# Replicating rows over partitions in a hybrid encoder layer: the DMA or GpSimd

## The chip, the cores and the metric

The kernel runs on one core of one Trainium2 chip. The metric is the device time of one execution in microseconds (us); lower is better.

## What is computed

One post-norm layer on 1024 tokens of 1024 features: an input norm, a mixer (forgetting attention beside a gated linear recurrence), a gated feed-forward, a gated per-layer embedding, with a norm behind each. The change touches the input norm and one term of the attention; the reference for these two, cut:

```python
def layer_norm(x, g, b):
    mu = mean(x, -1); var = mean((x - mu)**2, -1)
    return (x - mu) * rsqrt(var + 1e-5) * g + b

h = layer_norm(x, ln_in_g, ln_in_b)                # (1024 tokens, 1024)
q, k, v, f, ... = split(h @ w_in)
logf = log_sigmoid(f + b_forget)                   # (tokens, 8 heads)
c = cumsum(logf, axis=tokens)
logit[t, s] = q_t . k_s / sqrt(128) + c[t] - c[s]  # s <= t, per head
out = softmax(logit) @ v
```

Everything is float32. Products are taken as three products of rounded halves (a high and a low part of each operand).

## The kernel before

Tokens or features lie on the 128 partitions, in tiles of 128 by up to 1024. Three rows must be the same on every partition: the gain `g` and the bias `b` of the input norm (feature vectors, used with tokens on the partitions) and, for each of the 8 heads, `c[s]` along the keys (`CB[h]`, 1024 numbers). All three are made in the same way before the change: a DMA brings one row of 4 KB into partition 0, and GpSimd's `partition_broadcast` copies it to all 128.

The program runs in stages, in this order:

- **Input norm and v** (0 to about 170 us). `norm(i)` (L571) normalizes token tile i: VectorE takes the statistics (L425, L401), GpSimd the root (L403, L405, L412), VectorE applies mean, gain and bias to the first 512 features (L418, L419), ScalarE (L414) and GpSimd (L415, L416) to the others; TensorE then transposes the tile (`to_fm`, L432). While the first tiles come in, `ple` (L519) multiplies the per-layer embedding (lines 317 to 320, evicted by ScalarE at L526), 16 units over 8 PSUM banks.
- **Recurrence, merge gates, q and k** (to about 650 us): `winograd` (L340), block products in `product` (L331). `Weights` splits raw weights ahead: GpSimd forms sums of two blocks (`prep`, L108), ScalarE and VectorE round them into halves (L126, L127). `QueryKey.query` (L809) and `MergeGates` (L792) evict banks on VectorE.
- **Attention** (about 650 to 900 us), 8 heads in 4 steps of 256 queries, 32 steps in all (L1006). In a step, `probs_t` (L962) transposes the probabilities (L972, TensorE), `scores` (L927) computes the products of the step after the next one (L939 to L943), `pv` (L977) multiplies with v (L280 to L282), and `br_unit` (L989, products at L291 to L294) runs a product of the recurrent branch in between. In `scores`, VectorE subtracts `CB[h]` and takes the maximum (L944), ScalarE takes the exponential and its sum (L955), VectorE the reciprocal (L957), and GpSimd scales each row (L959), which the transposes wait for. `load_c(h + 1)` (L922) is called in the first step of head h.
- **Branch products, mixer out, feed-forward, embedding gate, norms** (about 900 us to the end). Later norms get their rows by a replicating DMA that GpSimd issues (lines 1107, 1258 and 1325).

The order on each engine is set by the tile framework, which simulates the program while it builds it and lets instructions pass each other where their dependences allow it. Each engine then runs its own list in order, and a waiting instruction holds all that stands behind it. SP issues nearly all loads and most stores, ScalarE the stores of a few results. Two things around the change matter: `rows` (L475) are two places in `f_mem`, of which the first, at 0 KB, is also the first place of the ring of raw v weights (`v_raw`, L487); and the tiles of `CB` (L861) take turns at 20 and 24 KB of `f_mem`, where the recurrence has held its `ur` and `sq` tiles before (L674, L675).

Of the kernel before, what the change touches and what calls it, by code (L numbers as in the profile page):

```python
# [15 lines left out]
P = 128  # L16
# [16 lines left out]
def pair_ops(pairs, ahead):  # L33
    """The operands of products of 2x2 blocks in Winograd's form of Strassen's algorithm, in the order of use."""
    ops = []
    for a, _ in pairs[:ahead]:
        ops += [(0, a), (1, a)]
    for n, (a, b) in enumerate(pairs):
        nxt = pairs[n + ahead][0] if n + ahead < len(pairs) else None
        ops += [("S1", a, b), ("S2", a, b), ("S4", a, b)]  # L40
        ops += [(0, nxt)] if nxt is not None else []
        ops.append(("S3", a, b))
        ops += [(1, nxt)] if nxt is not None else []
        ops.append(("n", b))
    return ops


class Weights:
    """Splits a sequence of stationary operands into rounded halves ahead of their use.

    An op is (kind, raw, raw). Kinds 0 and 1 are the contraction halves of a block, "n" is the negated second
    half, "S1" to "S4" are the sums of the halves of two blocks that Winograd's form needs.
    """
# [95 lines left out]
    def give(self, n):  # L149
        """Gives n places of raw weights away as they get free, in given."""  # L150
        self.wanted = n
# [6 lines left out]
class Feed:  # L158
    """Loads run ahead of their use by the ring of raw tiles; items: (source, what to do with the tile)."""
# [21 lines left out]
class Ring:  # L181
    """Tiles by turns; those of first come before them once."""
# [12 lines left out]
def trunk(ctx, tc, A, out):  # L195
# [29 lines left out]
    # On-chip memory, offsets in KB. Slots of 16 KB: 0 to 6 hold rounded halves, 7, 8 and the two parts of 9 are  # L225
    # typed by phase; f_mem is float32.
# [22 lines left out]
    def sv(s, off, *shape):  # L249
        """A view at off in slot s."""  # L250
        if s == 9:
            return view(flex["9a" if off < 8 else "9b"], off % 8, shape)
        return view(flex[s], off, shape) if s in flex else view(r_mem, 16 * s + off, shape)

    def blk(s):
        """The halves of a [512, 512] block in slot s."""
        return sv(s, 0, 4, 512), sv(s, 8, 4, 512)
# [8 lines left out]
    def xs_of(slots):  # L266
        """Operand (k, token chunk) of a [1024, 1024] activation whose blocks lie in slots[2 * chunk + k // 4]."""
        def x(k, t):
            hi, lo = blk(slots[2 * t + k // 4])
            return hi[:, k % 4, :], lo[:, k % 4, :]  # L270
        return x

    def toks_of(slots, i):
        """The operands over k for token tile i."""
        x, o = xs_of(slots), i % 4 * P
        return [tuple(a[:, o:o + P] for a in x(k, i // 4)) for k in range(KC)]

    def mm3(bank, w, x, first, last):
        """bank += w.T @ x for pairs of halves."""
        nc.tensor.matmul(bank, lhsT=w[0], rhs=x[0], start=first, stop=False)  # L280
        nc.tensor.matmul(bank, lhsT=w[0], rhs=x[1], start=False, stop=False)
        nc.tensor.matmul(bank, lhsT=w[1], rhs=x[0], start=False, stop=last)  # L282

    def gemm_fm(w, x, kc, tcs=(0, 1)):
        """[128 features, 512 tokens] per token chunk, with the weights stationary; w(k): halves."""
        out = [psum() for _ in tcs]
        for k in range(kc):
            wh, wl = w(k)
            for b, t in zip(out, tcs):
                xh, xl = x(k, t)  # L290
                nc.tensor.matmul(b, lhsT=wh, rhs=xh, start=(k == 0), stop=False)  # L291
                nc.tensor.matmul(b, lhsT=wh, rhs=xl, start=False, stop=False)  # L292
            for b, t in zip(out, tcs):
                nc.tensor.matmul(b, lhsT=wl, rhs=x(k, t)[0], start=False, stop=(k == kc - 1))  # L294
        return out
# [8 lines left out]
    def w_gemm(x):  # L304
        """The next block of the weights times x."""
        b = gemm_fm(ent(W.take(2)), x, KC)
        W.free(2)
        return b

    def gemm_tm(xs, ws, widths):  # L310
        """[128 tokens, width] per width, with the activations stationary; xs, ws: lists over k."""
        out = [psum() for _ in widths]
        n = len(xs)
        for k in range(n):
            (xh, xl), w = xs[k], ws[k]
            for b, (wh, wl), n_ in zip(out, w, widths):
                nc.tensor.matmul(b[:, :n_], lhsT=xh, rhs=wh, start=(k == 0), stop=False)  # L317
                nc.tensor.matmul(b[:, :n_], lhsT=xh, rhs=wl, start=False, stop=False)  # L318
            for b, (wh, wl), n_ in zip(out, w, widths):
                nc.tensor.matmul(b[:, :n_], lhsT=xl, rhs=wh, start=False, stop=(k == n - 1))  # L320
        return out

    def product(bank, s, first, nk=4):
        """bank += the next operand of the weights times the block of slot s."""
        (e,) = W.take(1)
        hi, lo = blk(s)
        for k in range(nk):
            w = e[:, k * P:(k + 1) * P], e[:, 512 + k * P:512 + (k + 1) * P]
            for j, (a, x) in enumerate(((w[0], hi), (w[0], lo), (w[1], hi))):
                start, stop = first and k == 0 and j == 0, k == nk - 1 and j == 2  # L330
                nc.tensor.matmul(bank, lhsT=a, rhs=x[:, k, :], start=start, stop=stop, skip_group_check=not first)  # L331
        W.free(1)
# [7 lines left out]
    def winograd(pairs, blocks, ahead, prologue, new_tile):  # L340
        """Products of 2x2 blocks with seven block products each; pairs: what to do with the sums.

        The banks are read as sums of products grow in them: c11 = x + y, c12 = x + z, c22 = x + the p5 of z, c21 = x.
        The last pair has the last two products in banks of their own, and their sums in a tile.
        """
# [52 lines left out]
    def norm_stats(st):  # L398
        """1/sqrt(var + eps) and the mean of the collected halves."""
# [8 lines left out]
    def normalize(y, rs, mu, g, b, cut):  # L408
        """y = (y - mu) * rs * g + b, VectorE up to cut, ScalarE and GpSimd from there."""
# [11 lines left out]
    def layer_norm(y, g, b, cut=512):  # L421
        """y = LN(y) * g + b over the free axis."""
# [5 lines left out]
    def to_fm(src, s, o):  # L428
        """Transposes src [128 tokens, 512] into the block of slot s, at token o."""
# [10 lines left out]
    def late_sums(y, j):  # L440
        """In place: B22 - B12 for y[j + 4]'s first half, B22 - B12 + B11 and that - B21 for y[j]'s halves."""
# [13 lines left out]
    def log_sigmoid(t, x, res):  # L455
        """res = min(x, 0) - log1p(exp(-|x|)), by the series of artanh; t: scratch."""
# [14 lines left out]
    # ---- input norm; v and the forget gates, token-major; the per-layer embedding's product while they come in  # L471
# [3 lines left out]
    rows = [fv(0, D), fv(18.75, D)]  # L475
    g, b = fv(10.75, D), fv(14.75, D)
    for row, nm in zip(rows, ("ln_in_g", "ln_in_b")):
        nc.scalar.dma_start(row[0:1], A[nm])
# [55 lines left out]
    load_x(0)  # L534
    p_raws += [load_ple(1, 1), load_ple(0, 1)]
# [4 lines left out]
    for row, t in zip(rows, (g, b)):  # L540
        nc.gpsimd.partition_broadcast(t, row[0:1])
# [18 lines left out]
    # the first recurrence waits for the memory that h leaves, the last is over before attention begins  # L560
# [88 lines left out]
    # sums of the blocks of h  # L649
# [19 lines left out]
    # ---- recurrence, merge gates, q and k  # L669
# [7 lines left out]
    class Recurrence:  # L677
# [63 lines left out]
        def decay(self):  # L741
            # log_a = ns4 * (1 + ta); 1 - a^2 = tanh(-log_a) * (1 + a^2); a in xc from here on
# [112 lines left out]
    # ---- attention; the recurrent branch out runs between its steps  # L855
# [11 lines left out]
    def attention_memory():  # L867
# [7 lines left out]
        load_c(0, fv(12, S)[0:1])  # L875
# [46 lines left out]
    def load_c(h, row):  # L922
        nc.sync.dma_start(row, c_dram[h, :])
        CB[h] = cb_tile()
        nc.gpsimd.partition_broadcast(CB[h], row)

    def scores(h, c):  # L927
        mx = sm.tile([P, 2], F32, tag="mx", name="mx")
        scs = []
        for r in range(2):  # L930
# [4 lines left out]
            for s0, w in ((0, L),) if L <= 512 else ((0, 512), (512, L - 512)):  # L935
                # products of fewer than 256 columns would not be faster
# [11 lines left out]
        # the row's maximum, then what the exponent adds to q.k - c_s: c_t - max  # L948
# [57 lines left out]
    for s, (h, c) in enumerate(steps):  # L1006
# [8 lines left out]
        if c == 0 and h + 1 < H:  # L1015
            load_c(h + 1, sv(9, 8, S)[0:1])

    # ---- attention branch out and merge
# [62 lines left out]
    # ---- mixer out, norm  # L1081
# [37 lines left out]
    # the weights of the first half are in the way of the later blocks  # L1119
# [11 lines left out]
    # ---- feed-forward, in  # L1131
# [50 lines left out]
    def fill_block(g, m, js=None):  # L1182
        """Block m of group g: B11, B21, B12 - B11, B22 - B12 + B11, B22, B22 - B12, B22 - B12 + B11 - B21."""
# [37 lines left out]
    # ---- feed-forward, out  # L1221
# [6 lines left out]
    def quads(gi, j):  # L1228
        """Accumulators of token tiles j and j + 4, per half of the features."""
# [6 lines left out]
    # the gate's weights, split by halves of the features: some take what the last group leaves of the blocks' slots,  # L1236
    # the rest comes in as its blocks are done with
# [83 lines left out]
    # ---- gated per-layer embedding, norm  # L1321
# [101 lines left out]
```

## Time and profile before

| what | value |
| --- | --- |
| time, median of 3 runs | 1920.08 us (1917.54 to 1923.84) |
| span of the profiled execution | 1915.1 us |
| TensorE busy | 1800.3 us, 94% |
| VectorE, ScalarE, GpSimd busy | 1211.2, 814.4, 716.0 us |
| mean granted clock of TensorE | 0.973 of full speed |
| HBM traffic | 121 GB/s over the span |

The span runs from the first to the last instruction of one execution; the page gives no time of that execution beside it. The three times lie 2.4 to 8.7 us above the span, and the median 5.0 us. TensorE is the engine that is busy nearly all the time, so what matters is where it is idle, for whom it waits there, and where its clock is not at full speed.

### The profile page before, as it was taken

The page shows a single profiled execution, that of the slowest core. Times are in us where ns is not written, and L with a number is a line of the kernel's source. Part 1 is how long each engine was busy: PE and PEld are TensorE (multiplying, and loading weights), DVE is VectorE, ACT ScalarE, POOL GpSimd, SP SyncE. Part 2 cuts the span into 40 slices and gives each one's busy share as a digit, 9 for nine tenths or more (in the row PEclk, how much of TensorE's full clock was granted, in tenths as well). Part 3 has the DMA queues.
Part 4 walks back from the last instruction along what each step waited for, and adds up shares of the span by engine and source line. Part 5 has one row for each costly group of instructions (what it writes and reads, how often), then busy time and mean ns, then how long its engine had stood idle before and what let it go on. Part 6 is the DMA issues. An engine that isn't in the chain of part 4 may idle for free. (4 is left out here: it accounts for less than half of the span.)

```text
span 1915.1 us, 23685 instructions
## 1 busy us (share of the span) xinstructions
PE 1800.3 (94%) x8556; PEld 1506.5 (79%) x8556; DVE 1211.2 (63%) x1800; ACT 814.4 (43%) x1420; POOL 716.0 (37%) x635
## 2 busy tenths in 40 slices
PE   6999999999999689889999999999999989898897
PEld 4998878888888477778888878888888768686686
DVE  5644767666666565556545585454545687979887
ACT  4424556555566454445422144333433343333322
POOL 3622222223222232232000463343433573646665
PEclk8999999999999889989999999999999999899998
DMA  6632232222323533323734124222222256464322
GB/s 232 259 114 74 80 119 92 98 91 97 118 89 121 176 102 112 107 91 123 253 133 176 45 92 139 87 81 87 81 85 88 66 179 206 158 202 160 118 77 77
DMA packets 119497, 233.96 MB, mean 122 GB/s; under 512 B 10946, under 2 KB 49986, under 8 KB 119380
## 3 DMA queue, kind: packets, MB, share of 16 engines
q1 hardware_dynamic: 102240, 205.70, 32.4%
q10 hardware_dynamic: 16132, 23.08, 3.3%
q0 software_dynamic: 1008, 3.67, 0.5%
q8 instruction: 67, 1.10, 0.2%
q14 instruction: 50, 0.41, 0.1%
HBM read 162.12 MB, written 70.29 MB: 121 GB/s over the span
## 5 line engine op out<-in xcount | busy, mean ns | idle before, releaser
L331 PE MATMUL bank<-r_mem,s 128*128 128x512 f32 x3261 | 773.6, 393 | 27.6 <-DVE f_mem L1271 9.9
L331 PEld LDWEIGHTS bank<-r_mem,s 128*128 128x128 f32 x3261 | 614.6, 189 | 160.6 <-issue 8.1
L108 POOL TENSOR_TENSOR f_mem<-f_mem 128x512 f32<-128x512 f32 (+1 forms) x232 | 333.6, 1449 | 645.5 <-DVE s L127 219.1
L127 DVE TENSOR_TENSOR s<-f_mem,s 128x512 fp32r<-128x512 f32 (+1 forms) x280 | 235.8, 854 | 143.7 <-ACT s L126 125.0
L126 ACT CAST s<-f_mem 128x512 fp32r<-128x512 f32 (+1 forms) x280 | 169.5, 618 | 338.2 <-PE bank L331 198.6
L331 PE MATMUL bank<-r_mem 128*128 128x512 f32 x1131 | 277.6, 394 | 14.2 <-DVE f_mem L1167 6.6
L331 PEld LDWEIGHTS bank<-r_mem 128*128 128x128 f32 x1131 | 214.4, 190 | 62.8 <-DVE f_mem L1167 7.0
L317 PE MATMUL bank<-r_mem 128*128 128x344 f32 (+2 forms) x389 | 138.7, 357 | 0.5 <-ACT f_mem L526 0.4
L318 PE MATMUL bank<-r_mem 128*128 128x344 f32 (+2 forms) x389 | 136.8, 352 | 0.0
L320 PE MATMUL bank<-r_mem 128*128 128x344 f32 (+2 forms) x389 | 133.5, 352 | 0.6 <-DVE r_mem L264 0.6
L126 ACT CAST r_mem<-f_mem 128x512 fp32r<-128x512 f32 (+1 forms) x100 | 60.0, 607 | 143.5 <-PE bank L331 87.0
L127 DVE TENSOR_TENSOR r_mem<-f_mem,r_mem 128x512 fp32r<-128x512 f32 (+1 forms) x100 | 92.0, 926 | 30.8 <-ACT r_mem L126 30.3
L291 PE MATMUL bank<-r_mem,s 128*128 128x512 f32 x224 | 87.8, 392 | 0.0
L292 PE MATMUL bank<-r_mem,s 128*128 128x512 f32 x224 | 87.3, 390 | 0.0
L1167 DVE TENSOR_TENSOR f_mem<-f_mem,bank 128x512 f32<-128x512 f32 x21 | 14.4, 687 | 113.4 <-PE bank L331 113.4
L959 POOL TENSOR_SCALAR f_mem<-f_mem,rinv 128x128 f32<-128x128 f32 (+3 forms) x64 | 49.3, 782 | 95.2 <-DVE rinv L957 50.8
L264 DVE TENSOR_TENSOR r_mem<-bank,r_mem 128x512 fp32r<-128x512 f32 (+2 forms) x120 | 67.5, 593 | 26.2 <-ACT r_mem L263 26.1
L263 ACT CAST r_mem<-bank 128x512 fp32r<-128x512 f32 (+2 forms) x120 | 57.4, 518 | 61.0 <-PE bank L972 31.5
L294 PE MATMUL bank<-r_mem,s 128*128 128x512 f32 x224 | 82.2, 390 | 0.0
L317 PEld LDWEIGHTS bank<-r_mem 128*128 128x128 f32 x389 | 73.1, 188 | 8.3 <-ACT f_mem L526 0.8
L320 PEld LDWEIGHTS bank<-r_mem 128*128 128x128 f32 x389 | 73.1, 188 | 8.2 <-DVE r_mem L264 0.9
L318 PEld LDWEIGHTS bank<-r_mem 128*128 128x128 f32 x389 | 73.1, 188 | 7.0
(280 smaller groups left out, 3037.2 us busy)
## 6 DMA issues: line engine op xcount, KB each, us to landing
f_mem<-in_w_fg SPq DMA_DIRECT2D x22, 512.0 KB, 3.9
f_mem<-in_w_fu SPq DMA_DIRECT2D x22, 512.0 KB, 3.1
act_dram<-f_mem SPq DMA_DIRECT2D x43, 256.0 KB, 2.3
f_mem<-act_dram SPq DMA_DIRECT2D x16, 512.0 KB, 4.4
y_dram<-f_mem SPq DMA_DIRECT2D x32, 256.0 KB, 4.4
f_mem<-y_dram SPq DMA_DIRECT2D x26, 256.0 KB, 2.5
s<-in_w_ffn_out SPq DMA_DIRECT2D x12, 512.0 KB
f_mem<-in_w_ffn_out SPq DMA_DIRECT2D x10, 512.0 KB, 5.6
```

The lines of the kernel that those rows point to most:

```text
L108: self.nc.gpsimd.tensor_tensor(out, x, y, op=op)
L126: nc.scalar.copy(hi, src)
L127: nc.vector.tensor_tensor(lo, src, hi.bitcast(F32), op=ALU.subtract)
L263: nc.scalar.copy(hi, src)
L264: (eng or nc.vector).tensor_tensor(lo, src, hi.bitcast(F32), op=ALU.subtract)
L291: nc.tensor.matmul(b, lhsT=wh, rhs=xh, start=(k == 0), stop=False)
L292: nc.tensor.matmul(b, lhsT=wh, rhs=xl, start=False, stop=False)
L294: nc.tensor.matmul(b, lhsT=wl, rhs=x(k, t)[0], start=False, stop=(k == kc - 1))
L317: nc.tensor.matmul(b[:, :n_], lhsT=xh, rhs=wh, start=(k == 0), stop=False)
L318: nc.tensor.matmul(b[:, :n_], lhsT=xh, rhs=wl, start=False, stop=False)
L320: nc.tensor.matmul(b[:, :n_], lhsT=xl, rhs=wh, start=False, stop=(k == n - 1))
L331: nc.tensor.matmul(bank, lhsT=a, rhs=x[:, k, :], start=start, stop=stop, skip_group_check=not first)
```

## The change

The row of partition 0 and the copy by GpSimd go. One DMA for each row, with a source that repeats the row 128 times, writes all partitions: 512 KB into SBUF in place of 4 KB. For `g` and `b` ScalarE issues it, now behind `load_x(0)`; for `CB[h]` SP does. The rest of the diff takes out comments, and line numbers shift by up to 4.

```diff
     hs = (0, 1, 2, 3)
-    rows = [fv(0, D), fv(18.75, D)]
     g, b = fv(10.75, D), fv(14.75, D)
-    for row, nm in zip(rows, ("ln_in_g", "ln_in_b")):
-        nc.scalar.dma_start(row[0:1], A[nm])
...
     load_x(0)
+    for t, nm in ((g, "ln_in_g"), (b, "ln_in_b")):
+        nc.scalar.dma_start(t, A[nm].partition_broadcast(P))
...
-    for row, t in zip(rows, (g, b)):
-        nc.gpsimd.partition_broadcast(t, row[0:1])
...
-        load_c(0, fv(12, S)[0:1])
+        load_c(0)
...
-    def load_c(h, row):
-        nc.sync.dma_start(row, c_dram[h, :])
+    def load_c(h):
         CB[h] = cb_tile()
-        nc.gpsimd.partition_broadcast(CB[h], row)
+        nc.sync.dma_start(CB[h], c_dram[h, :].partition_broadcast(P))
...
         if c == 0 and h + 1 < H:
-            load_c(h + 1, sv(9, 8, S)[0:1])
+            load_c(h + 1)
```

The order changes in two stretches, the first 70 us and the attention; behind the attention it is the same row by row. On GpSimd each broadcast stood between two rows of the sequencer without operands ("ISA"), which the trace calls MODIFY_POOL_CONFIG. One head before, from GpSimd's list (L959 scales probabilities):

```order
L959 TENSOR_SCALAR f_mem<-f_mem,rinv 128x512
L925 ISA
L925 ISA f_mem<-s9b 128x1024
L959 ISA
L959 TENSOR_SCALAR f_mem<-f_mem,rinv 128x640
```

The same place now (the scaling is at L955 in the changed file):

```order
L955 TENSOR_SCALAR f_mem<-f_mem,rinv 128x512
L955 TENSOR_SCALAR f_mem<-f_mem,rinv 128x640
L955 TENSOR_SCALAR f_mem<-f_mem,rinv 128x768
```

All three rows are gone, there and at the other broadcasts; no such pair of rows is left anywhere behind the constants.

SP's list where the attention's first row is loaded, before (L762 stores the recurrence, L171 loads an operand of the attention):

```order
L824 DMA k_dram<-s9b 128x512
L923 DMA f_mem<-c_dram 1x1024
L762 DMA rnn_dram<-f_mem 128x512
L762 DMA rnn_dram<-f_mem 128x512
L171 DMA s9a<-v_dram 128x8x128
```

And now (the load of `CB` is at L921):

```order
L821 DMA k_dram<-s9b 128x512
L759 DMA rnn_dram<-f_mem 128x512
L759 DMA rnn_dram<-f_mem 128x512
L921 DMA f_mem<-c_dram 128x1024
L171 DMA s9a<-v_dram 128x8x128
```

The load stands behind the two stores of the recurrence, which read the place that it writes, and ahead of the load of v.

TensorE's list in one attention step before (L972 transposes, L280 to L282 are products with v, L942 and L943 end the scores of a later step):

```order
L972 MATMUL bank<-ident,f_mem 128x128 x4
L942 MATMUL bank<-r_mem 128x256
L943 MATMUL bank<-r_mem 128x256
L942 MATMUL bank<-r_mem 128x256
L943 MATMUL bank<-r_mem 128x256
L280 MATMUL bank<-r_mem 128x256
L972 MATMUL bank<-ident,f_mem 128x128 x7
```

The same scores now (L938 and L939 end them, L968 transposes):

```order
L968 MATMUL bank<-ident,f_mem 128x128 x4
L281 MATMUL bank<-r_mem 128x256
L282 MATMUL bank<-r_mem 128x256
L280 MATMUL bank<-r_mem 128x256
L281 MATMUL bank<-r_mem 128x256
L282 MATMUL bank<-r_mem 128x256
L935 MATMUL bank<-r_mem 128x384
L937 LDWEIGHTS b_mem
L937 MATMUL bank<-b_mem 128x128
L938 MATMUL bank<-r_mem 128x256
L939 MATMUL bank<-r_mem 128x256
```

The last products of these scores have moved behind the transposes of the step and behind most of its products with v.

## Rows read from the trace of the kernel before

**Rows 1.** Page: busy time of each engine; granted clock in 40 slices.
```profile
PE 1800.3 (94%) x8556; PEld 1506.5 (79%) x8556; DVE 1211.2 (63%) x1800; ACT 814.4 (43%) x1420; POOL 716.0 (37%) x635
...
PEclk8999999999999889989999999999999999899998
```

**Rows 2.** Waits, PE, 600 to 900 us: total us, times, longest.
```profile
PE bank L972 <- POOL f_mem L959: 27.6, 6, 6.8
PE bank L331 <- DVE s9b L792: 6.4, 1, 6.4
PE bank L939 <- DVE mx L944: 3.7, 2, 3.2
PE bank L331 <- DVE s9b L809: 2.6, 1, 2.6
```

**Rows 3.** Timeline, GpSimd, 685 to 750 us: start, us, operation, idle before and its releaser.
```profile
697.12 1.30 POOL L925 PARTITION_BROADCAST f_mem<-s9b  x1 [5.86 <-DVE mx L944]
705.26 3.77 POOL L959 TENSOR_SCALAR f_mem<-f_mem,rinv 128x640 f32<-128x640 f32 x4 [6.84 <-DVE r_mem L264]
...
740.57 3.77 POOL L959 TENSOR_SCALAR f_mem<-f_mem,rinv 128x640 f32<-128x640 f32 x4 [7.05 <-issue]
```

**Rows 4.** Windows: length, busy PE, PEld, DVE, ACT, POOL, clock, DMA share, GB/s.
```profile
600.00:900.00 300.00, 256.03 (x1447) 218.77 (x1446) 178.81 (x463) 152.74 (x330) 83.53 (x138) 0.91 0.37 121
...
860.00:900.00 40.00, 39.38 (x251) 34.10 (x249) 26.60 (x76) 21.92 (x50) 10.93 (x22) 1.00 0.33 109
```

**Rows 5.** Windows of low clock, 600 to 900 us: first, last, sum of eight.
```profile
631.00:641.75 10.75, 6.21 (x15) 4.87 (x16) 5.47 (x16) 4.88 (x10) 4.28 (x7) 0.52 0.24 75
...
857.00:859.70 2.70, 2.64 (x13) 2.65 (x14) 0.87 (x2) 1.07 (x2) 2.70 (x8) 0.50 0.00 0
sum 44.35, PE 38.65 PEld 33.74 DVE 25.04 ACT 21.03 POOL 24.18; mean PE 4.83 PEld 4.22 DVE 3.13 ACT 2.63 POOL 3.02
```

**Rows 6.** Timeline, first row load of the attention and its readers.
```profile
612.81 0.92 SPq L762 DMA_DIRECT2D rnn_dram<-f_mem  x2
...
623.94 0.42 DVE L944 CUSTOM_DVE_ANT_0 f_mem<-bank,f_mem 128x256 f32<-128x256 f32 x1 [7.06 <-POOL f_mem L925]
...
631.03 2.48 POOL L108 TENSOR_TENSOR f_mem<-f_mem 128x512 f32<-128x512 f32 x2 [7.13 <-issue]
```

**Rows 7.** DMA issues of the whole run: times, KB each, us to landing.
```profile
rnn_dram<-f_mem SPq DMA_DIRECT2D x16, 256.0 KB, 2.2
...
f_mem<-in_ln_ffn_b POOLq DMA_DIRECT2D x1, 512.0 KB, 7.4
s<-in_b_ple_gate POOLq DMA_DIRECT2D x1, 512.0 KB, 4.0
```

**Rows 8.** Timeline, VectorE: end of head 1's scores, begin of head 3's.
```profile
696.22 0.74 DVE L944 CUSTOM_DVE_ANT_0 f_mem<-bank,f_mem,mx 128x512 f32<-128x512 f32 x1
...
743.53 0.29 DVE L944 CUSTOM_DVE_ANT_0 f_mem<-bank,f_mem 128x128 f32<-128x128 f32 x1 [5.09 <-PE bank L943]
```

**Rows 9.** Timeline, GpSimd and SP, the first 27 us.
```profile
10.89 2.48 POOL L541 PARTITION_BROADCAST f_mem<-f_mem  x2 [9.33 <-issue]
12.22 0.81 SPq L493 DMA_DIRECT2D f_mem<-in_w_v  x2
...
24.69 0.18 POOL L403 TENSOR_SCALAR ve<-mv 128x1 f32<-128x1 f32 x1 [11.32 <-issue]
```

**Rows 10.** Waits, PE, 0 to 60 us.
```profile
PE bank L317 <- ACT s L263: 8.5, 1, 8.5
PE bank L432 <- ACT f_mem L526: 7.0, 1, 7.0
PE bank L432 <- POOL s9a L416: 1.7, 2, 1.1
```

**Rows 11.** Windows at the start, columns as in Rows 4.
```profile
5.00:10.00 5.00, 1.54 (x4) 1.25 (x5) 2.78 (x3) 2.14 (x3) 0.00 (x0) 1.00 0.97 363
...
28.90:37.10 8.20, 7.08 (x20) 5.59 (x21) 6.98 (x9) 6.13 (x9) 3.12 (x5) 0.50 0.77 249
```

## The prediction

> **What bounds the kernel now.** I read the page first: TensorE is busy 94% of the span, and its granted clock is at 8 tenths in the first of 40 slices and in three between 622 and 862 us (a slice is 47.9 us) [rows 1]. So time can be won only where TensorE is idle or slow. The windows came next: between 600 and 900 us it is busy 256.0 of 300 us, so 44.0 us are idle [rows 4]. The list of TensorE's waits says for whom: 27.6 us, in six pieces, its transposes wait for GpSimd's scaling of the probabilities (L959), and 12.7 us more are three lines that wait for VectorE [rows 2].
>
> Why is GpSimd late? Its timeline shows it for one head. The broadcast itself takes 1.30 us and ends at 698.42, but the scaling behind it begins at 705.26; the 6.84 us between are empty, and VectorE's L264, named as the releaser, isn't an input of the scaling. One head on, the same stretch is 7.05 us and put down to "issue", a wait for nothing that the profile shows [rows 3]. So each broadcast costs GpSimd an empty stretch behind it, besides one ahead of it: 7.1 us for VectorE's first subtraction (L944), which waits for the broadcast, and then again 7.13 us before the next sum of weights (L108) [rows 6]. I take both for a change of GpSimd's program, to the broadcast and back. The Trainium skill (GPSIMD Engine Reference, 2.1 Instruction dispatch) says that the first call of a freshly loaded kernel costs about 6 us which no instruction in the profile shows. The trace agrees in kind but is longer, and has it on the way back as well; by the page's figure each such stretch would be about 1 us shorter, and the forecast some 6 us smaller.
>
> TensorE's idle stretches have a second price: behind them its granted clock is 0.5, the lower of its levels (1.2 instead of 2.4 GHz). Eight windows between 600 and 900 us hold this, at a mean of 0.50 to 0.55; TensorE is busy 38.65 us in them [rows 5].
>
> The start shows the same. The first broadcast waits 9.33 us for "issue", and the first root of the norm (L403) another 11.32 us [rows 9]. TensorE has used up its PSUM banks by then and idles 7.0 us for an eviction (L526) that stands on ScalarE behind the norm, then 1.1 us for GpSimd [rows 10], and runs at 0.50 until 37.1 us [rows 11].
>
> **The change, part by part.**
>
> *Attention, what goes.* No row that changes GpSimd's program is left in its list. The idle time that hangs on the broadcasts is 27.6 + 6.4 + 2.6, and of the 3.7 the longest piece, 3.2: 39.8 us [rows 2]. The work done at low clock takes half as long at full: 38.65 x (1 - 0.52) = 18.6 us [rows 5]. Together 58.4 us, if nothing else is late there.
>
> *Attention, what is late next.* The last head has no broadcast in it, and from 860 to 900 us TensorE is busy 39.38 of 40 us at clock 1.00, with VectorE at 26.6 and ScalarE at 21.9 [rows 4]. That is the nearest row for what remains: 0.6 us for each of seven heads, 4.3 us. Where the recurrence ends and the attention begins more engines are close to full; I keep 3 us there, an estimate between 0 and the 10 us of the two idle pieces that stand at that place (3.2 and 6.8) [rows 2].
>
> *The eight loads.* Each moves 512 KB instead of 4. Loads of this kind exist: the norms' rows land 4.0 to 7.4 us after their issue [rows 7]. The first can't be issued before the recurrence's second store has been read, which is issued at about 613.4 [rows 6] and takes 2.2 us [rows 7]; so issue at about 616 and landing at 620.2 to 623.7, against 623.94 now, when L944 starts [rows 6]. VectorE is held until then, and behind L944 stand the evictions at L809 and L792. So of the 2.6 us at L809 0 to 2 us stay, I take 0.7; the 6.4 us at L792 go, since they come from L108, and that no longer waits. Behind this load on SP stand the loads of v and of the recurrence; they start some tenths of a us later, beside work. The later loads have room: head 3's tile is free when head 1's last scores have been read, at 697, and is first read at 743.5 [rows 8], 46 us, or about 40 after the shrinking, for a landing of at most 7.4. I cost them at nothing; the cover is that lead. So 58.4 - 4.3 - 3 - 0.7 = 50.4, and I say 50.
>
> *The start.* Won: 7.0 + 1.1 idle [rows 10], and half of the 7.08 us at clock 0.50, 3.5 [rows 11]: 11.6 us. Also the first v weights no longer wait on SP for the row's place, so that load and the seven loads queued behind it (three tiles of x, four constants) can be issued at about 4 instead of 12.2 us [rows 9]. Lost: two loads of 512 KB, 1.05 MB, come beside those that TensorE's first product waits 8.5 us for [rows 10]. With the engines at 0.97 and 363 GB/s [rows 11] that is 2.9 us if all of it goes ahead, 0 if none does; the first load is issued with the first of SP's and the second only behind ScalarE's first copy, so I take three quarters, 2.2. The Trainium skill (DMA: Bandwidth & Descriptors, Rules for kernel authors) speaks against a free ride: issuing from several engines doesn't add bandwidth, because all use the same 16 DMA engines and interleave. By that rule alone all 2.9 us would be lost, and the forecast 0.7 us later; the trace before can't show it, its two loads there being of 4 KB. Later on the DMA must give the same data some 8 us earlier; between 30 and 60 us it was busy most of the time, so 0 to 4 us may come back as waits, and I take 1.5. So 11.6 - 2.2 - 1.5 = 7.9, say 8 (bounds 4.7 and 11.6).
>
> *Behind the attention* the order is unchanged, and nothing is won or lost.
>
> **The sum.** 50 + 8 = 58 us off the span of 1915.1: 1857. The median lies 5.0 us above that span, so 1920.1 - 58 = 1862 us. Best case, nothing is kept back: 58.4 + 11.6 = 70, 1850. With 2 us kept in each of eight heads and the lower bound of the start: 42.4 + 4.7 = 47, 1873.
>
> **The rivals.**
>
> *VectorE or ScalarE becomes the bound.* If the attention's 300 us shrink to 250, VectorE is busy 178.8 of them, 72%, and ScalarE 61% [rows 4]. Both work in order, and their bursts may hold TensorE where GpSimd did. If half of the attention's gain goes that way, 25 + 8 = 33 us remain: 1887. Against it stands the last head, full at 66% of VectorE. Chance 0.14, spread over 1876 to 1912.
>
> *Slower: the scores come too late.* The new order puts the last products of a step's scores behind that step's transposes and most of its products with v. From there the maximum, the exponential, the sum and GpSimd's scaling must be over before the transposes two steps on. If that chain no longer fits, TensorE waits in all 32 steps, not in eight places. It decides from 58 / 32 = 1.8 us a step; at 2.2 us a step the time is 1920 - 58 + 70 = 1932. For it speaks that TensorE's list is what moved most; against it, that steps before the change without a broadcast show almost no wait, and that two steps of about 9 us are a long time for that chain. Chance 0.05.
>
> *It doesn't take the stalls away*, because GpSimd changes its program for another reason too, or because each stall only hid a wait for something else, as long: 1920. The list shows no such change left, and the stall's end is GpSimd's own start. Chance 0.03.
>
> **How the numbers follow.** The forecast as summed, 1846 to 1876, has 0.78, and its middle is 1862. The range 1848 to 1886 leaves out its lower rim, two thirds of the first rival and the other two: about 0.2. A measurement of this kernel can tell 0.3%, 5.8 us, from no change. Faster by more: 0.78 + 0.14 = 0.92; within: 0.03; slower: 0.05.
>
> **What would show it.** Right: no broadcast on GpSimd and no empty stretch of 7 us there; TensorE's wait at the transposes for the scaling below 5 us; clock 1.00 from 60 to 900 us; the 7.0 us at L432 gone and TensorE's first product at 10 to 11 us instead of 8.5; the attention's end 55 to 60 us earlier. Wrong: L944 waiting for a load of `CB`; TensorE waiting for VectorE or ScalarE at the transposes or the scores in most steps; the first product later than 12 us; or a gap left near 625 to 635 us.

## The result

The changed kernel takes 1861.9 us (median of 4 runs, 1861.4 to 1866.0); the kernel before took 1920.2 on the same chip (4 runs). The ratio is 0.970, its 95% interval 0.968 to 0.972. The forecast was 1862. The profiled execution after has a span of 1859.9 us, against 1915.1 before.

The first rows of the page after answer to [rows 1]:

```profile
PE 1785.9 (96%) x8556; PEld 1496.4 (80%) x8556; DVE 1212.0 (65%) x1800; ACT 811.2 (44%) x1420; POOL 706.2 (38%) x625
...
PEclk9999999999999999999999999999999999899999
```

TensorE executes as many matmuls as before in 14.4 us less busy time, because most of the low clock at the start and between 622 and 862 us is gone. GpSimd has ten instructions fewer, the ten broadcasts, and saves only 9.8 us of busy time by it: what the change wins isn't the work of the broadcasts.

TensorE's waits from 600 to 900 us, with total, times and longest, answer to [rows 2]; the attention now ends at 872.6 us, so the stretch holds all of it:

```profile
PE bank L968 <- POOL f_mem L955: 1.7, 2, 1.1
PE bank L280 <- ACT r_mem L263: 1.3, 1, 1.3
PE bank L968 <- DVE f_mem L384: 1.0, 1, 1.0
PE bank L935 <- DVE mx L940: 0.7, 2, 0.5
```

L968 and L955 are the lines that were L972 and L959. The 27.6 us in which the transposes waited for the scaling are 1.7, and the two waits for `s9b` are gone. The window over the same 300 us (columns as in [rows 4]) holds 7.1 us of idle TensorE instead of 44.0, and a clock of 0.98 instead of 0.91:

```profile
600.00:900.00 300.00, 292.86 (x1707) 250.31 (x1706) 206.59 (x519) 171.23 (x371) 78.78 (x132) 0.98 0.53 172
```

GpSimd's timeline in head 3, the place that [rows 3] show of before. There is no broadcast, and the long idle piece ahead of the scaling ends with VectorE's `rinv`, which is an input of it: GpSimd is early here and waits for its data.

```profile
692.68 2.28 POOL L955 TENSOR_SCALAR f_mem<-f_mem,rinv 128x384 f32<-128x384 f32 x2
703.70 1.71 POOL L955 TENSOR_SCALAR f_mem<-f_mem,rinv 128x640 f32<-128x640 f32 x2 [8.75 <-DVE rinv L953]
706.65 2.12 POOL L955 TENSOR_SCALAR f_mem<-f_mem,rinv 128x896 f32<-128x896 f32 x2 [1.24 <-DVE rinv L953]
```

The eight row loads stand in the list of DMA issues (number, KB each, median us to landing), beside those of [rows 7]:

```profile
f_mem<-c_dram SPq DMA_DIRECT2D x8, 512.0 KB, 5.6
```

At the start, TensorE's waits from 0 to 60 us answer to [rows 10]. The 7.0 us for the eviction are gone, the first product comes 2.3 us later (10.72 instead of 8.46), and the other waits at the transposes (L432) are 4.2 us instead of 1.7:

```profile
PE bank L317 <- ACT s L263: 10.7, 1, 10.7
PE bank L432 <- POOL s9a L416: 3.0, 1, 3.0
PE bank L432 <- issue: 1.2, 1, 1.2
```

Four places in the two traces divide the gain. The first product of a weight block (L331, line number unchanged) begins at 141.6 us instead of 147.8: 6.2 us from the start. The recurrence's last store is issued at 606.4 instead of 613.4: 7.0. The attention's last eviction (L980, before L984) begins at 872.6 instead of 928.9: 56.3, so 49.3 from the attention. The last store of the output is issued at 1857.2 instead of 1912.4: 55.2, by which the span is shorter too.

### The profile page after: what moved, and what is told of

It is laid out like the page before. It is cut to its first block, busy times and chain, and to the rows that moved or that the text cites. A ratio compares the mean times of both kernels' runs of the same rounds, so it can differ in the third digit from the quotient of the medians.

```text
span 1859.9 us, 23625 instructions
## 1 busy us (share of the span) xinstructions
PE 1785.9 (96%) x8556; PEld 1496.4 (80%) x8556; DVE 1212.0 (65%) x1800; ACT 811.2 (44%) x1420; POOL 706.2 (38%) x625
## 5 line engine op out<-in xcount | busy, mean ns | idle before, releaser
L331 PE MATMUL bank<-r_mem,s 128*128 128x512 f32 x3261 | 770.4, 392 | 18.1 <-DVE f_mem L1267 9.9
L331 PEld LDWEIGHTS bank<-r_mem,s 128*128 128x128 f32 x3261 | 613.2, 189 | 149.3 <-issue 8.0
L331 PE MATMUL bank<-r_mem 128*128 128x512 f32 x1131 | 277.5, 395 | 14.4 <-DVE f_mem L1163 6.6
L331 PEld LDWEIGHTS bank<-r_mem 128*128 128x128 f32 x1131 | 214.5, 190 | 62.8 <-DVE f_mem L1163 7.0
L127 DVE TENSOR_TENSOR r_mem<-f_mem,r_mem 128x512 fp32r<-128x512 f32 (+1 forms) x100 | 92.2, 928 | 31.0 <-ACT r_mem L126 30.5
L955 POOL TENSOR_SCALAR f_mem<-f_mem,rinv 128x128 f32<-128x128 f32 (+3 forms) x64 | 54.6, 866 | 127.4 <-DVE rinv L953 119.2
L1163 DVE TENSOR_TENSOR f_mem<-f_mem,bank 128x512 f32<-128x512 f32 x21 | 14.4, 687 | 113.4 <-PE bank L331 113.4
L264 DVE TENSOR_TENSOR r_mem<-bank,r_mem 128x512 fp32r<-128x512 f32 (+2 forms) x120 | 67.8, 593 | 23.9 <-ACT r_mem L263 23.9
```

What stands on the lines that cost most here:

```text
L127: nc.vector.tensor_tensor(lo, src, hi.bitcast(F32), op=ALU.subtract)
L264: (eng or nc.vector).tensor_tensor(lo, src, hi.bitcast(F32), op=ALU.subtract)
```

## The experiments

The theory was that GpSimd's change to a broadcast and back is what costs: each broadcast has an empty stretch on both sides, and TensorE waits behind it and then runs at the lower clock. Rivals were the broadcast's own work and its readers' wait for it, the new order of instructions in the lists of the engines, and any wait of GpSimd for a row's load, whatever comes behind it. Eight of the ten runs are the changed kernel with one thing added or moved. In those with broadcasts of 128 x 8 elements into a tile that nobody reads, and in the one with an ordinary operation in their place, the lists of TensorE, VectorE, ScalarE and SP are row for row those of the changed kernel.

### One half of the change at a time

Only the start: the kernel before, with `g` and `b` by replicating loads.

```
-    for row, nm in zip(rows, ("ln_in_g", "ln_in_b")):
-        nc.scalar.dma_start(row[0:1], A[nm])
+    for t, nm in ((g, "ln_in_g"), (b, "ln_in_b")):
+        nc.scalar.dma_start(t, A[nm].partition_broadcast(P))
...
-    for row, t in zip(rows, (g, b)):
-        nc.gpsimd.partition_broadcast(t, row[0:1])
```

> Only the gain and the bias of the input norm come by the replicating DMA; the eight rows of the attention are still copied by GpSimd. If the gain of the two parts adds up as the sum said, this one gives the start's part: the first block product begins 6 us earlier than before (147.8 in the kernel before, 141.6 after), and the time is 1914 us (1910 to 1916). The attention's gaps stay: TensorE waits some 27 us at its transposes for GpSimd's scaling. If it is the new order of the instructions that gained most, the time is well below 1900, since the order of the attention moves here too.

Measured: 1918.3 us, ratio 0.999 (0.998 to 1.001), no change that can be told, and 2 us above the range that was expected. The start gave what it should: the first block product stands at 142.7 us and the recurrence's last store at 607.9, 5.1 and 5.5 us earlier than before. But the attention ends at 928.8, as before. It lasts 320.9 us instead of 315.5. Its waits, 560 to 940 us:

```profile
PE bank L969 <- POOL f_mem L956: 33.6, 6, 9.8
PE bank L331 <- DVE s9b L789: 6.6, 1, 6.6
```

The wait for the scaling is 6 us more than in [rows 2]. This kernel's attention isn't in the order of before: some 160 of its matmuls stand elsewhere in TensorE's list. Whether the order did it or the attention takes up any earlier start was open; the last two runs below bear on it.

Only the attention: the kernel before, with the rows of the log forget gates by replicating loads.

```
-        nc.sync.dma_start(row, c_dram[h, :])
         CB[h] = cb_tile()
-        nc.gpsimd.partition_broadcast(CB[h], row)
+        nc.sync.dma_start(CB[h], c_dram[h, :].partition_broadcast(P))
```

> Only the eight rows of the attention come by the replicating DMA; the start is as before. By the sum the attention gives 50 us: 1870 us (1866 to 1875), with TensorE's idle 7 us at 22 to 29 us still there. If the two parts share their gain, or the start's gain is given back later, it is nearer to 1862.

Measured: 1872.7 us, ratio 0.975 (0.974 to 0.977). The attention lasts 271.8 us instead of 315.5, and the start keeps its wait for the eviction (8.7 us here). So the attention carries most of the gain, as expected. Against the 1919.3 us of before in this comparison the two halves alone give 1.0 and 46.6 us, and both together gave 58.3, so they can't be added; each of the three kernels has a list of its own in the attention.

### The eight broadcasts back, tiny and unread

```
         nc.sync.dma_start(CB[h], c_dram[h, :].partition_broadcast(P))
+        nc.gpsimd.partition_broadcast(junk, CB[h][0:1, :8])
```

> The changed kernel with one more GpSimd instruction for each head: a partition broadcast of 8 numbers of CB[h] into a tile that nobody reads. TensorE, VectorE, ScalarE and SP have the same lists, row by row, as the changed kernel; only GpSimd's has the eight broadcasts and the two rows without operands around each. If the empty stretches around a broadcast are the cost, whatever it copies, most of the attention's 50 us come back: 1900 to 1910 us, GpSimd with empty stretches of 7 us behind each broadcast, and TensorE waiting over 20 us at its transposes for the scaling. If the copy itself (1.3 us for 1024 numbers) or the wait of its readers was the cost, under 10 us come back: 1862 to 1872. If the order was what gained, nothing comes back: 1862.

Measured: 1920.7 us, ratio 1.000 (0.999 to 1.002). Eight operations that write 32 bytes to each partition and that nobody waits for undo the whole gain, 11 us more than the most that was expected. The attention ends at 933.3 us, 60.7 later than in the changed kernel. GpSimd's timeline in head 3, and TensorE's waits from 560 to 960 us (L957 is the scaling, L970 the transposes):

```profile
698.18 0.28 POOL L923 PARTITION_BROADCAST junk<-f_mem  x1 [6.66 <-DVE r_mem L264]
705.66 2.11 POOL L957 TENSOR_SCALAR f_mem<-f_mem,rinv 128x896 f32<-128x896 f32 x2 [7.20 <-issue]
```

```profile
PE bank L970 <- POOL f_mem L957: 51.4, 6, 13.2
PE bank L280 <- ACT r_mem L263: 1.6, 1, 1.6
PE bank L970 <- DVE f_mem L384: 1.3, 1, 1.3
```

The broadcast itself takes 0.28 us instead of 1.30 [rows 3], and the empty stretches are the same, 6.66 and 7.20 us. The longest wait, 13.2 us, is near to both stretches of one broadcast together (6.66 + 0.28 + 7.20 = 14.1). So the price is the change there and back, not the copy, not the readers' wait for it, and not the new order, which this kernel has.

### An ordinary operation instead, two broadcasts, and half of them

One operation of the scaling's kind on 128 x 8 elements in each head:

```
+        nc.gpsimd.tensor_scalar(junk, CB[h][:, :8], 1.0, 1.0, op0=ALU.mult, op1=ALU.mult)
```

> The changed kernel plus one ordinary GpSimd operation per head (a tensor_scalar of 128 x 8 elements of the replicated row into a tile that nobody reads), at the place where the eight tiny broadcasts of the run before stood. TensorE's, VectorE's, ScalarE's and SP's lists are those of the changed kernel row for row. Theory (what costs the 60 us is that a broadcast is another kind of work for GpSimd, and the change there and back): nothing happens, 1862 within 2 us, and no empty stretch of 7 us around the added operation. Rival (any eighth instruction that waits there for the row's load holds GpSimd up, whatever its kind): GpSimd stands still until the row has landed, some 3.6 to 6 us a head, 30 to 50 us in all: 1890 to 1910.

Measured: 1865.7 us, ratio 0.972 (0.971 to 0.974), 3.7 us above the 1862 that were expected within 2. The group of these operations (count, busy time and mean, idle time ahead):

```profile
L923 POOL TENSOR_SCALAR junk<-f_mem 128x8 f32<-128x8 f32 x8 | 2.3, 286 | 16.9 <-DMA f_mem<-c_dram 15.7 <-PE bank L294 1.1
```

GpSimd does wait for the loads here, 15.7 us in the eight heads together, and TensorE waits 3.2 us for the scaling instead of 1.7. The attention ends 2.9 us later than in the changed kernel, 1.2 of which are already there at the first block product. That is not the 30 to 50 us of the rival: a wait for a load is cheap, a broadcast isn't.

Two tiny broadcasts in each head:

```
+        for _ in range(2):
+            nc.gpsimd.partition_broadcast(junk, CB[h][0:1, :8])
```

> The changed kernel plus two tiny broadcasts per head, one right behind the other, into the tile that nobody reads; the other engines' lists are those of the changed kernel. If the price lies in the change of GpSimd's work to broadcasts and back, the second one of a pair comes within 1 us of the first and the whole takes what it took with one per head: 1920, at most 1928 (8 x 1 us more). If each broadcast has its own empty stretch ahead, 8 x 6 to 7 us come on top: 1965 to 1980.

Measured: 1942.2 us, ratio 1.012 (1.011 to 1.014). This is between the two expectations, and the timeline says why. In six heads the two stayed together; in two the order put an operation of the scaling between them. One head of each sort:

```profile
660.34 0.28 POOL L924 PARTITION_BROADCAST junk<-f_mem  x1 [6.06 <-issue]
667.32 2.10 POOL L958 TENSOR_SCALAR f_mem<-f_mem,rinv 128x896 f32<-128x896 f32 x2 [6.69 <-issue]
675.17 0.28 POOL L924 PARTITION_BROADCAST junk<-f_mem  x1 [5.75 <-PE bank L281]
683.01 0.82 POOL L958 TENSOR_SCALAR f_mem<-f_mem,rinv 128x128 f32<-128x128 f32 x2 [7.56 <-issue]
...
708.76 0.64 POOL L924 PARTITION_BROADCAST junk<-f_mem  x2 [6.34 <-issue]
716.87 2.10 POOL L958 TENSOR_SCALAR f_mem<-f_mem,rinv 128x896 f32<-128x896 f32 x2 [7.48 <-issue]
```

Two that follow each other take 0.64 us together and have one stretch ahead and one behind. Two with a scaling between them have all four. Against the kernel with one broadcast in a head, the broadcasts of heads 0 to 2 begin 0.5, 0.6 and 1.5 us later; that of head 3, which comes behind the divided pair, 10.6 us; those of heads 4 to 7, 11.8 to 12.0; and the attention's end, behind the second divided pair, 20.3 (953.6 against 933.3). So the six that follow another one cost next to nothing, and the two more changes there and back cost 9.1 us (10.6 - 1.5) and some 8.4 (20.3 - 11.9). GpSimd's list of instructions shows what the timeline leaves out: a bare instruction stands ahead of each broadcast or pair and another one behind it. The same two heads in the list:

```
L924 ISA
L924 ISA junk<-f_mem 128x8
L958 ISA
L958 TENSOR_SCALAR f_mem<-f_mem,rinv 128x896
L958 TENSOR_SCALAR f_mem<-f_mem,rinv 128x1024
L924 ISA
L924 ISA junk<-f_mem 128x8
L958 ISA
...
L924 ISA
L924 ISA junk<-f_mem 128x8 x2
L958 ISA
```

One tiny broadcast in heads 1, 3, 5 and 7 only:

```
+        if h % 2:
+            nc.gpsimd.partition_broadcast(junk, CB[h][0:1, :8])
```

> The changed kernel plus one tiny broadcast in heads 1, 3, 5 and 7 only. The other engines' lists are those of the changed kernel. If each broadcast has a price of its own (59 us for eight, 7.3 us for one), 1862 + 29 = 1891, within 4 us. If the price is a matter of all heads together (stalls that add up only from one head to the next, or a clock that falls only when stalls are frequent), the time is nearer to one of the ends, under 1880 or over 1903.

Measured: 1893.5 us, ratio 0.987 (0.985 to 0.988). The attention ends 30.5 us later than in the changed kernel, 1.3 of which come from the start: 29.2 / 4 = 7.3 us for one broadcast, where eight took 60.7 / 8 = 7.6. Each has a price of its own, and the prices add up.

### The loads once more

In each head but the first the row is loaded a second time, into a place that nobody reads.

```
+        if h:
+            nc.sync.dma_start(sv(9, 8, S), c_dram[h, :].partition_broadcast(P))
```

> The changed kernel with each head's row, from the second head on, loaded twice: a second replicating DMA of 512 KB brings it to a place that nobody reads. I costed these loads at nothing: 1862 us, within 3. If the loads compete with others that the attention waits for, seven more loads at 1.4 us each (512 KB at 363 GB/s) cost up to 10 us: 1872.

Measured: 1868.0 us, ratio 0.973 (0.971 to 0.975). The attention ends 6.3 us later than in the changed kernel, with 11.5 us of idle TensorE in it (606 to 879 us) instead of 7.1 (606 to 873). But some 110 matmuls stand elsewhere in TensorE's list, and other orders alone go with differences as large: the run with only the attention changed has no broadcast there either, and its attention lasts 5.6 us longer than that of the changed kernel (271.8 against 266.2). So the 6 us can't be put down to the seven more loads of 512 KB; what these cost stays open.

### The start

`g` and `b` loaded from SP's queue behind the first four loads, instead of from ScalarE's ahead of its first copy:

```
-    for t, nm in ((g, "ln_in_g"), (b, "ln_in_b")):
-        nc.scalar.dma_start(t, A[nm].partition_broadcast(P))
     p_raws += [load_ple(1, 1), load_ple(0, 1)]
+    for t, nm in ((g, "ln_in_g"), (b, "ln_in_b")):
+        nc.sync.dma_start(t, A[nm].partition_broadcast(P))
```

> The changed kernel with the two replicating loads of g and b issued by SP behind the four loads of the per-layer embedding, instead of by ScalarE ahead of its first copy and of w_v. The changed kernel's first product stands at 10.72 us, that of before at 8.46: if the replicating loads ahead of the first operands are what delays it, it goes back to 8.5 to 9 us and the time to 1860, within 1 us, with the 7.0 us wait for the broadcasts still gone. If the delay has another cause, the first product stays at 10.7 us. If g and b now land too late for the first normalization, the wait at the transposes (line 432) grows instead by what the start gives, and the time is 1862 or more.

Measured: 1863.0 us, ratio 0.971 (0.969 to 0.972), no better than the changed kernel. TensorE's waits, 0 to 60 us:

```profile
PE bank L317 <- ACT s L263: 8.1, 1, 8.1
PE bank L432 <- issue: 7.2, 1, 7.2
```

The first product comes at 8.07 us, so the replicating loads ahead of the first operands are what delays it. But the first block product stands at 142.3 us, 0.7 later than in the changed kernel: TensorE does its first products earlier and then waits longer at the transposes of the normalized rows. What ends the start in this run is the input norm, not the first product. The first rows are normalized no later than in the changed kernel (VectorE ends L419 at 14.6 us, there at 15.6), but the statistics of the next ones (L425) begin at 24.9 us instead of 23.3, behind a rounding (L264) for which VectorE stood idle 8.8 us. The lists of the engines moved here too, so what the 2.3 us are worth in the order of the changed kernel isn't shown.

One tiny broadcast at the start, ahead of GpSimd's first operation of the norm:

```
     nc.gpsimd.memset(mhalf, -0.5)
+    junk = const.tile([P, 8], F32, name="junk")
+    nc.gpsimd.partition_broadcast(junk, b[0:1, :8])
```

> The changed kernel plus one tiny broadcast (128 x 8 elements from the row of b) on GpSimd at the start, ahead of its first operation of the input norm, into a tile that nobody reads. The other engines' lists are those of the changed kernel row for row. The run with only g and b loaded by replicating loads had its first block product 5 us earlier than before and ended no earlier. Theory: a stall at the start shifts everything behind it, so this one costs what that start had won, 5 to 7 us at the first block product and at the end: 1867 to 1869. Rival: what the start wins or loses is taken up later (by a wait further on that doesn't move): first block product 5 to 7 us later, the end within 2 us of 1862.

Measured: 1871.2 us (1868.7 to 1873.1), ratio 0.975 (0.972 to 0.979); the profiled execution's span is 1866.9, 7.0 more than that of the changed kernel, while the medians lie 9.3 apart, 2 us more than expected. GpSimd's timeline shows the stretches of [rows 9] again:

```profile
10.80 0.47 POOL L540 PARTITION_BROADCAST junk<-f_mem  x1 [9.23 <-issue]
20.22 0.18 POOL L403 TENSOR_SCALAR ve<-mv 128x1 f32<-128x1 f32 x1 [8.95 <-issue]
```

The first block product is 6.4 us late (147.99), the attention's end 7.2 (879.9), the span's end 7.0. A stall at the start goes through to the end.

That one and the eight in attention together:

> The tiny broadcast at the start and the eight tiny broadcasts in attention together, on the changed kernel's lists. With the eight alone the time was 1920.7. If the stalls at the start and in attention add up, 1920.7 plus what the one at the start costs alone (5 to 7 us): 1926 to 1928, and the missing gain of the run with g and b alone came from its other order of instructions in attention. If attention takes the start's loss up as long as its broadcasts are there, 1920 to 1922.

Measured: 1927.6 us (1922.2 to 1930.7), ratio 1.004 (1.003 to 1.005). The kernel with the eight alone took 1920.7, so the start's broadcast costs 6.8 us here too (10.1 by the spans of the profiled executions, 1928.8 and 1918.7; in this one the empty stretch behind it is longer, 10.24 us, and the norm's first step begins at 22.3 instead of 20.2). The stalls at the start and in the attention add up as long as the order stays. That bears on the first run: its start's gain wasn't taken up by the stalls as such, which leaves the other order of its attention; the order wasn't tried by itself.

This run shows one thing more. It has nine tiny broadcasts in the order of the changed kernel and is slower than the kernel before with its ten large ones, 1920.8 in the same comparison. Counted by changes that isn't odd. In the kernel before, the broadcasts of heads 1 and 2 follow each other with no ordinary operation between them, and so do those of `g` and `b` [rows 9]:

```profile
660.94 1.69 POOL L925 PARTITION_BROADCAST f_mem<-s9b  x1 [14.18 <-ACT f_mem L955]
664.14 1.79 POOL L925 PARTITION_BROADCAST f_mem<-s9b  x1 [1.51 <-DMA s9b<-c_dram]
673.94 1.68 POOL L959 TENSOR_SCALAR f_mem<-f_mem,rinv 128x640 f32<-128x640 f32 x2 [8.01 <-issue]
```

Between the two there is 1.51 us, for a load, and no stretch of 6 to 8. So the ten broadcasts of before are eight changes there and back, seven of them in the attention; the run with eight tiny ones has eight as well and takes the same time, and this one has nine and takes 6.8 us more. Against the attention of the changed kernel (266.2 us), one change costs 7.0 us with the seven of before (315.5), 7.5 with the eight tiny ones (326.3), and 7.8 with the seven of the first run (320.9). Of the 10.8 us by which the attention with eight tiny broadcasts is longer than that of before, the eighth change is 7.5; the rest, some 3 us, can be the order or the edit itself and stays open.

## Why the prediction was right

**The mechanism** was as said. An empty stretch lies on each side of a broadcast, it doesn't depend on the broadcast's size, it is paid once for two that follow each other, and an ordinary operation in the same place doesn't have it. The Trainium skill (GPSIMD Engine Reference, 2.1 Instruction dispatch) gives about 6 us for the first call of a freshly loaded kernel, with no instruction in the profile to show it. With one tiny broadcast in each head the stretches ahead are 5.8 to 6.7 us in seven of the eight heads (10.5 in the other), and 5.8 to 6.0 in five, as the page has it; those behind are 7.1 to 8.1. So ahead of a broadcast the page's figure fits these rows, where the prediction had called the trace longer; what it doesn't have is the way back. By these rows the price falls due at every change, and on the way back as well. One thing in the mechanism was put too broadly: not each broadcast has a stretch on both sides. Two pairs of before follow each other directly, so that its ten broadcasts are eight changes. The sum wasn't hurt by it, since it went by the idle time of [rows 2] and not by a count.

**The sum** met the time to the microsecond, and that was luck in part. By the spans 58 us were forecast and 55.2 measured (1915.1 to 1859.9): the start gave 6.2 instead of 8, the recurrence 0.8 more, the attention 49.3 instead of 50, and 1.1 were lost behind it. The 2.8 us that are missing came back by the last term, the 5.0 us from span to median. After the change the median lies only 2.0 us above the span (1861.9 and 1859.9). Wherever time and span of the same execution are both known, the time is 1.7 to 2.4 us longer; so the span of 1915.1 very likely belongs to the fastest of the three executions before (1917.5), and the 5.0 held some 3 us by which the others were slower. The medians differ by 58.3 us.

**What is late next** was sized well in the part that is idle and wrongly in the part that is clock. From 600 to 900 us 7.1 us of idle time are left, where the steps added up to 4.3 + 3 + 0.7 = 8.0. But "the work done at low clock takes half as long at full", 18.6 us, took all of it as won, and 13.6 were: in windows cut where the clock changes, 5.1 us of the 18.7 are still lost. Two of these windows after, with the idle piece ahead of the first (columns as in [rows 4]):

```profile
633.00:636.00 3.00, 0.74 (x4) 0.20 (x2) 3.00 (x6) 2.88 (x7) 0.00 (x0) 1.00 1.02 320
636.00:642.50 6.50, 6.41 (x21) 5.01 (x22) 4.84 (x17) 2.00 (x4) 0.00 (x0) 0.50 0.89 330
653.00:656.70 3.70, 3.70 (x18) 3.56 (x19) 3.59 (x10) 2.51 (x7) 1.62 (x5) 0.54 0.48 148
```

From 633 to 636 us TensorE is busy 0.74 of 3 us while VectorE and ScalarE are full: it is the place where recurrence and attention meet, at which 3 us had been kept. TensorE waits there 0.97 us for VectorE and 1.34 us for ScalarE. It reaches into the place, "near 625 to 635 us", at which the prediction had named a gap as a sign of being wrong; with 2.3 us in all it stays within the 3 that were kept. Behind it the clock is 0.50 for 6.5 us. "Clock 1.00 from 60 to 900 us" was therefore wrong. The attention came to 49.3 us, against 50, because more idle time went than the steps said (36.9 us instead of 39.8 - 8.0 = 31.8; they had counted only 39.8 of the 44.0 us as hanging on the broadcasts) and less of the low clock (13.6 instead of 18.6). That this came out right was luck: two terms were off by 5 us each, in opposite directions. Their sum, 50.5, is 1.2 above the 49.3; the windows hold more than the attention.

**The first row's load** is issued at 608.5 us, 2.1 behind the store, as the steps put it (there 616 on the clock of before, with the store at 613.4). No wait of L940 for a load of `CB` stands among VectorE's waits of the attention; the largest group of them from 600 to 640 us is 5.1 us for ScalarE in rounding (L264). **The later loads** at nothing: in the changed kernel no wait for them shows; what a doubling of them costs isn't shown, since the run that tried it changed the order too.

**The start** was forecast at 8 and gave 6.2. The 2.2 us for the first product were hit (10.72 against 8.46 us), though not by the steps' reason: the second load doesn't wait for ScalarE's first copy but is issued at 1.22 us, and the copy begins at 2.45. The run from SP's queue speaks against adding it to the sum as it stands: without it the first block product comes no earlier there. Of the loads that should go out at about 4 us only the two of `w_v` did (4.47 and later); the three tiles of x were issued at 8.5 to 10.0 us and the constants from 10.9 on, but no term hung on it. What was mis-sized is what the stall's end would bring, 11.6 us. TensorE now has a gap from 30.9 to 35.1 us, and half clock behind it:

```profile
30.90:35.10 4.20, 0.65 (x5) 0.44 (x5) 2.78 (x3) 1.26 (x2) 4.02 (x6) 1.00 0.82 324
35.00:38.60 3.60, 3.52 (x11) 2.94 (x12) 3.03 (x2) 3.24 (x6) 3.60 (x4) 0.54 0.56 214
```

GpSimd is busy 4.02 of the 4.2 us with the norm of the next rows of x, which it got late: its root's first step (L403) waits until 27.4 us for VectorE's L401, which has rounding (L264) ahead of it in its list. The 1.5 us kept for the density of the DMA stand for no wait that shows.

The Trainium skill (DMA: Bandwidth & Descriptors, Rules for kernel authors) says that issuing from several engines adds no bandwidth. By the page alone all 2.9 us of the two loads, an estimate from [rows 11], would have been lost at the first product; 2.3 were. That agrees in kind: loads from ScalarE's queue delay those that SP has issued. ScalarE's rounding of the first operand waits for its load until 8.46 us, where it began at 4.94 before and begins at 5.01 in the run from SP's queue:

```profile
8.46 2.21 ACT L263 CAST s<-f_mem 128x1024 fp32r<-128x1024 f32 x2 [5.62 <-DMA f_mem<-in_pT]
```

**Behind the attention** 1.1 of the 56.3 us are lost by the last store, where nothing had been expected. From the attention's last eviction to the last store it is 983.5 us before and 984.6 after; in the other ten traces it lies between 982.7 and 986.6, so the 1.1 us don't stand out from what traces differ by.

**The rivals.** VectorE or ScalarE as the bound: VectorE is busy 206.6 of the 300 us, and TensorE 292.9, so no. The scores too late in TensorE's list: its largest group of waits at the scores (L935) is 0.7 us. No effect: the run with eight tiny broadcasts back is what that would have looked like. That the stalls would cost much more in the new order isn't shown: per change it is 7.5 us there and 7.0 in the old one.

## What to carry to other kernels

On GpSimd, count the changes between a partition broadcast and ordinary work, not the elements: in this attention, where TensorE waits behind GpSimd, a change for 128 x 8 elements cost 7.3 to 7.6 us of the program's time on average, and for 128 x 1024 it cost 7.0. If a broadcast can't be replaced by a replicating load with lead time (5.6 us for 512 KB here), put two that belong together directly behind each other: the second one then cost next to nothing. And a partial change that moves the order of instructions can't be priced by subtraction: put the suspected operation back into the final order, in a form that nobody waits for, and compare.

## What the runs showed of the hardware that wasn't expected

That the price falls due at each change, and not at each broadcast or by its size, is shown above. At the start the stretches are longer, beside loads that keep the DMA busy: 9.2 and 9.3 us ahead and 9.0 and 10.2 behind in the two runs with a tiny broadcast there. Whether the loads make them longer wasn't tried. A row of the sequencer like those around a broadcast doesn't cost such a stretch everywhere: one stands ahead of the mask of the constants too, and there GpSimd's operation begins at 1.03 us, right behind one that ends at 0.98. What moves in such a stretch stays open: the queues for instructions carry the same 67 and 50 packets in the profiles of before and after, so it doesn't show there.

The granted clock was at its lower level, 0.50, behind a stretch in which TensorE was busy 0.74 of 3 us, with idle pieces of 0.97 and 1.34 us as the longest waits in it; the steps had counted only the long stalls of before as its cause.
